# Where three kinds of sums are made: operands of a last product, weights' sums by DMA, and gated branch adds

## Chip, cores and metric

The kernel runs on one core of a Trainium2 chip. The metric is device time in microseconds, the median of three runs: 1693.74 us (1692.67 to 1696.91). All times below are microseconds (us) unless marked ns; times within an execution count from the start of its span.

## What is computed

Two layers of a transformer block over 512 tokens of width 1024, in float32. Each layer has a mixer of four branches (three kinds of attention and a retention), gated and summed, and then a gated feed-forward product:

```
h = rms_norm(x, g_pre_mix[l])
branches = stack(o_a, o_b, o_c, o_d)            # (S, 4, 256)
gates = sigmoid(h @ w_gate).reshape(S, 4, 1024)
merged = sum(einsum('snw,nwd->snd', branches, w_branch) * gates, axis=1)
x = x + rms_norm(merged @ w_out, g_post_mix[l])
h = rms_norm(x, g_pre_ffn[l])
f = (silu(h @ w_ffn_gate[l]) * (h @ w_ffn_up[l])) @ w_ffn_down[l]
x = x + rms_norm(f, g_post_ffn[l])
```

## The kernel before

**Matmuls in three.** Every float32 matrix is split into a high part in TensorE's own float format and a low part, the remainder. ScalarE casts the high part, VectorE (in a few places GpSimd) subtracts to get the low one, and TensorE does three matmuls: high by high, high by low, low by high. Weights come from HBM by DMA into `raw` tiles and are split into `whi` and `wlo`, four buffers each, two steps ahead of their use: `conversion` (lines 289 and 290) for most, `plain` (lines 403 and 404) in the feed-forward stage. Activations are split by `split_to` (lines 520 and 521, or 523 and 524 where a factor is applied).

**The gates** (`gates`). For each layer there are four groups, one per branch (`gi` 0 to 3), each with four pairs of 128 output columns (`dp` 0 to 3). A pair is two gate products of 24 matmuls, each followed by a multiplication on VectorE (line 1299) and a tanh on ScalarE (line 1300), and then two branch products of 6 matmuls. Their results are taken by line 1319 on VectorE, in place in the tanh's tile, and added to `merged` on GpSimd (line 1320). In the fourth group `merged` is final, and it is split at once for the output product (lines 523 and 524).

**Sums of weights** (`make_sums`). The last layer's down product, 2816 by 1024, is computed as a 2 by 2 block product with seven block products in place of eight. That needs four sums of weight blocks, p, r, q and v, for each of six k steps (`LAST_K`: five of two 128-row tiles, one of one). They are made in DRAM by DMAs that GpSimd issues, two for each sum: one copies (line 361), one adds (line 362), and q starts from p, v from q. Ahead of p and of r a DMA of one element (line 360) reads the tanh's tile just made, so that the sums start no earlier than that. One step's sums are made in each group with `gi` above 0, at its first pair: steps 0 to 2 in layer 0, 3 to 5 in layer 1 (step 5 is half as large). GpSimd issues in order, so its adds of line 1320 stand in one queue with these DMAs.

**The last product** (`finish`). It does the seven block products, P0 to P6 here, in six k steps each. The operands are quarters of the hidden matrix `h` (22 tiles; `FH` is 11) or sums of quarters. P0 takes one, P1 one, P2 the first sums (t1), P3 one, P4 the second sums (t2), P5 the third (t3), P6 the fourth (t4). `beside` makes t1 while P1 runs and t2 while P3 runs (lines 1753 and 1757, eleven adds each on 128 by 256). Those of t3 and t4 are made in `of_t3` and `of_t4` (lines 1783 and 1790), just ahead of the split of the same operand, which `operands(OPS)` calls three steps ahead of use. Each product has 66 matmuls (`block`, lines 1889 to 1891) into two banks, one for each 128 tokens of a half; the last two steps (`k` from `LATE` on) are done for the first bank and then for the second. P0, P4, P5 and P6 add into the same two banks, and so do P2 and P3 in two others. After a product, a copy on ScalarE (line 1837) takes each bank, VectorE adds it to another product's result (lines 1839, 1842, 1845), and `done` squares it (line 1815, with a sum), scales it (line 1817) and, at the end of a token's row, makes a root (`root`, line 551, for which ScalarE loads another function table) and writes the output (line 1828).

**The order of the work.** In the stages of the change no order is written by hand: a scheduler sets each engine's order when the program is built, and each engine then runs its instructions in that order, waiting where an operand or a buffer is not ready.

Of the kernel before, what the change touches and what calls it, by code (L numbers as in the profile page):

```python
# [13 lines left out]
ALU = mybir.AluOpType  # L14
# [22 lines left out]
HALF = (slice(0, 256), slice(256, 512))  # L37
# [18 lines left out]
FH = FT // 2  # L56
# [151 lines left out]
class Builder:  # L208
# [137 lines left out]
        return [self.ap["wts"][self.woff[i + j]:self.woff[i + j + 1]].rearrange("(p n) -> p n", p=128)  # L346
                for j in range(len(LAST_K))]

    def make_sums(self, j, when):

        dma = self.nc.gpsimd.dma_start
        a11, a12, a21, a22 = (self.block_quarter(n)[j] for n in range(4))
        n = a11.shape[1]
        for name, first, more in (("p", a21, a22), ("r", a11, a21), ("q", None, a11), ("v", None, a12)):
            d = self.dram.tile([128, n], F32, tag="%s%d" % (name, j), name="sums")
            self.sums[name, j] = d
            if first is None:
                first = self.sums["p" if name == "q" else "q", j]
            else:
                dma(d[0:1, 0:1], when[0:1, 0:1])  # L360
            dma(d, first, max_dma_last_dim=1024)
            dma(d, more, accum_op=ALU.add, max_dma_last_dim=1024)

# [926 lines left out]
    def gates(self, l, u):  # L1290
        nc = self.nc
        merged = [None] * 8
        for gi, n in enumerate(GATE_ORDER):
            for dp in range(4):
                ts = []
                for d in range(2):
                    ps = yield from self.fm("gate", u)
                    z = self.a()
                    nc.vector.tensor_mul(z, ps, self.rB)  # L1299
                    nc.scalar.activation(z, z, AF.Tanh, scale=0.5)  # L1300
                    ts.append(z)
                    if d == 0 and dp == 0 and gi > 0:
                        self.make_sums(3 * l + gi - 1, z)
                    yield 3
                if dp == 0:
                    self.drain("b%d" % n)
                br = self.br[n]
                w = self.take("branch")
                for d in range(2):
                    ps = self.ps("acc")  # L1310
                    for k in range(2):
                        self.mm3(ps, (w[0][2 * d + k], w[1][2 * d + k]), br[k], k == 0, k == 1)
                    dd = 2 * dp + d
                    if gi == 0:
                        merged[dd] = self.a()
                        nc.vector.scalar_tensor_tensor(merged[dd], ts[d], 1.0, ps, op0=ALU.add, op1=ALU.mult)
                    else:
                        t = ts[d]
                        nc.vector.scalar_tensor_tensor(t, t, 1.0, ps, op0=ALU.add, op1=ALU.mult)
                        nc.gpsimd.tensor_add(merged[dd], merged[dd], t)  # L1320
                    if gi == 3:
                        merged[dd] = self.split(merged[dd], scale=0.5)
                yield 12
        return merged
# [408 lines left out]
    def finish(self, h):  # L1733

        nc = self.nc
        h0, h1 = HALF
        mm = nc.tensor.matmul
        stt = nc.vector.scalar_tensor_tensor
        gout = [self.a(), self.a()]
        for i in range(2):  # L1740
            nc.sync.dma_start(gout[i], self.ap["gout"][:, 512 * i:512 * i + 512])
        t1, t2 = [None] * FH, [None] * FH
        row = lambda k: (k // 2, HALF[k % 2])

        def total(dst, k, f):

            i, hs = row(k)
            if k % 2 == 0:
                dst[i] = self.a()
            f(dst[i][:, hs])  # L1750
# [10 lines left out]
        def split(src, n):  # L1761
            hi, lo = self.ar(), self.ar()
            self.split_to(hi[:, :n], lo[:, :n], src[:, :n])
            return hi, lo

        def plain(k0, hs):
            def f(k, nk):
                hi, lo = self.ar(), self.ar()
                for i in range(nk):
                    self.split_to(hi[:, HALF[i]], lo[:, HALF[i]], h[k0 + k + i][:, hs])  # L1770
                return hi, lo
            return f

        def of_t1(k, nk):
            return split(t1[k // 2], 256 * nk)

        def of_t2(k, nk):
            return split(t2[k // 2], 256 * nk)

        def of_t3(k, nk):  # L1780
            t = self.a()
            for i in range(nk):
                nc.vector.tensor_sub(t[:, HALF[i]], h[FH + k + i][:, h1], h[k + i][:, h1])
                h[k + i] = None
            return split(t, 256 * nk)

        def of_t4(k, nk):
            t = self.a()
            for i in range(nk):
                stt(t[:, HALF[i]], t2[k // 2][:, HALF[i]], -1.0, h[FH + k + i][:, h0], op0=ALU.mult, op1=ALU.subtract)  # L1790
            t2[k // 2] = None
            return split(t, 256 * nk)

        products = (plain(0, h0), plain(FH, h0), of_t1, plain(FH, h1), of_t2, of_t3, of_t4)

        beside = {1: make_t1, 3: make_t2}
        todo = deque((f, k, nk) for f in products for k, nk in LAST_K)
        ready = deque()

# [212 lines left out]
```

## Time and profile before

| what | value |
|---|---|
| median of three runs | 1693.74 us (1692.67 to 1696.91) |
| profiled execution, own time | 1688.88 us |
| its span, first to last instruction | 1687.1 us |
| TensorE matmul (PE) busy | 1650.9 us, 98% |
| VectorE (DVE) busy | 1132.2 us, 67% |
| ScalarE (ACT) busy | 851.2 us, 50% |
| GpSimd (POOL) busy | 376.1 us, 22% |
| mean granted TensorE clock | 0.997 |

The profiled execution is a single one, with its own time beside the span. PE is matmul time, and matmuls overlap a little, so their starts say more than their durations. Issuing a DMA is not counted as busy. A wait is put down to the engine that came last by the profile; where that engine was itself held, the cause is one link further back.

### The profile page before, as it was taken

Reading aid. Unit: us, or ns where it says so; the run is one execution under the profiler, and the core shown is the slowest. Engines: PE = TensorE matmul, PEld = TensorE weight load, DVE = VectorE, ACT = ScalarE, POOL = GpSimd, SP = SyncE. Lnnn points to the kernel's source line nnn. Section 1 sums busy time; section 2 is a strip of 40 time slices with the busy share of each in tenths; the row PEclk is TensorE's granted clock in tenths of the full one; section 3 lists DMA queues with packets and bytes.
Section 4 is the critical chain, followed back from the end, with each engine's and each line's share of the span. In section 5 each row is a group of like instructions: output and inputs, shape, how many; then the busy total and the mean of one; then the engine's idle time right before and its main releaser. Section 6 shows DMA issues by size and latency. Waiting matters only on the chain.

```text
span 1687.1 us, 26433 instructions
## 1 busy us (share of the span) xinstructions
PE 1650.9 (98%) x9746; PEld 1460.2 (87%) x9746; DVE 1132.2 (67%) x2149; ACT 851.2 (50%) x1680; POOL 376.1 (22%) x404
## 2 busy tenths in 40 slices
PE   9999999999999999999999999999999999999997
PEld 7788888888798999988887888888888989999875
DVE  6667777644569777762286577675445687777987
ACT  6566553323455555553265665533334565555664
POOL 0145333332230000000121453334332300010000
PEclk9999999999999999999999999999999999999998
DMA  5644325776625777343236343257755257775561
GB/s 198 178 107 127 93 82 185 171 191 157 201 82 146 182 184 183 101 152 101 76 128 181 104 130 90 84 176 179 192 142 174 65 150 193 184 186 150 189 238 68
DMA packets 93313, 248.88 MB, mean 148 GB/s; under 512 B 11136, under 2 KB 22656, under 8 KB 93184
## 3 DMA queue, kind: packets, MB, share of 16 engines
q1 hardware_dynamic: 72768, 205.24, 38.8%
q0 software_dynamic: 20416, 41.95, 13.4%
q8 instruction: 77, 1.26, 0.3%
q14 instruction: 52, 0.43, 0.1%
HBM read 220.93 MB, written 31.46 MB: 150 GB/s over the span
## 4 chain that ended last, share of the span: by engine, by line
PE 59%; DVE 5%; ACT 2%; issue 1%; DMA 1%; POOL 1%; DVEq 0%; SPq 0%; ACTq 0%
PE acc L528 8%; PE acc L529 8%; PE acc L530 8%; PE acc L502 4%; PE acc L504 4%; PE acc L503 4%; PE b L504 3%; PE b L503 3%; PE b L502 3%; PE b L1889 1%; PE b L1891 1%; PE b L1890 1%; PE b L751 1%; DVE wlo L290 1%; PE b L671 1%
## 5 line engine op out<-in xcount | busy, mean ns | idle before, releaser
L528 PE MATMUL acc<-a,whi 128*128 128x512 f32 (+1 forms) x1238 | 477.8, 386 | 3.0 <-DVE a L1299 3.0
L530 PE MATMUL acc<-a,wlo 128*128 128x512 f32 (+1 forms) x1238 | 469.0, 379 | 0.0
L529 PE MATMUL acc<-a,whi 128*128 128x512 f32 (+1 forms) x1211 | 458.6, 379 | 0.0
L290 DVE TENSOR_TENSOR wlo<-raw,whi 128x512 fp32r<-128x512 f32 (+3 forms) x398 | 279.0, 732 | 134.1 <-ACT whi L289 133.3
L289 ACT CAST whi<-raw 128x512 fp32r<-128x512 f32 (+3 forms) x398 | 213.0, 576 | 305.8 <-PE acc L529 155.9
L530 PEld LDWEIGHTS acc<-a,wlo 128*128 128x128 f32 x1238 | 233.0, 188 | 44.0 <-issue 0.5
L528 PEld LDWEIGHTS acc<-a,whi 128*128 128x128 f32 x1238 | 233.9, 189 | 42.5 <-ACT whi L289 3.8
L529 PEld LDWEIGHTS acc<-a,whi 128*128 128x128 f32 x1211 | 228.5, 189 | 38.9 <-DVE a L524 0.6
L404 DVE TENSOR_TENSOR wlo<-raw,whi 128x1024 fp32r<-128x1024 f32 x132 | 157.6, 1195 | 71.2 <-ACT whi L403 67.7
L403 ACT CAST whi<-raw 128x1024 fp32r<-128x1024 f32 x132 | 135.4, 1027 | 122.7 <-PE acc L503 51.1
L502 PE MATMUL acc<-a,whi 128*128 128x256 f32 x560 | 158.6, 283 | 1.9 <-DVE a L1638 1.5
L503 PE MATMUL acc<-a,whi 128*128 128x256 f32 x560 | 158.4, 283 | 0.0
L504 PE MATMUL acc<-a,wlo 128*128 128x256 f32 x560 | 158.3, 283 | 0.0
L502 PE MATMUL b<-a,whi 128*128 128x256 f32 x448 | 126.8, 283 | 0.0
L503 PE MATMUL b<-a,whi 128*128 128x256 f32 x448 | 126.8, 283 | 0.0
L504 PE MATMUL b<-a,wlo 128*128 128x256 f32 x448 | 126.8, 283 | 0.0
L1299 DVE TENSOR_TENSOR a<-acc,a 128x512 f32<-128x512 f32 x64 | 44.1, 689 | 111.4 <-PE acc L530 111.4
L520 ACT CAST a<-a 128x512 fp32r<-128x512 f32 (+1 forms) x143 | 77.6, 567 | 74.7 <-DVE a L859 18.0
L333 POOL DMA_DIRECT2D raw<-wts x36 | 31.6, 877 | 350.1 <-DMA raw<-wts 129.0
L502 PEld LDWEIGHTS acc<-a,whi 128*128 128x128 f32 x560 | 107.4, 192 | 2.3 <-ACT whi L403 1.7
L503 PEld LDWEIGHTS acc<-a,whi 128*128 128x128 f32 x560 | 107.5, 192 | 0.1
L504 PEld LDWEIGHTS acc<-a,wlo 128*128 128x128 f32 x560 | 107.4, 192 | 0.0
(280 smaller groups left out, 3237.7 us busy)
## 6 DMA issues: line engine op xcount, KB each, us to landing
raw<-wts SPq DMA_DIRECT2D x257, 512.0 KB, 3.9
raw<-wts POOLq DMA_DIRECT2D x36, 512.0 KB, 6.5
a<-a SPq DMA_DIRECT2D x120, 128.0 KB, 2.3
sums<-wts POOLq DMA_DIRECT2D x30, 512.0 KB, 7.3
raw<-sums SPq DMA_DIRECT2D x20, 512.0 KB, 3.9
raw<-wts SPq DMA_DIRECT2D x35, 256.0 KB, 2.9
sums<-sums POOLq DMA_DIRECT2D x10, 512.0 KB, 4.6
a<-xT SPq DMA_DIRECT2D x16, 256.0 KB, 5.4
```

The lines of the kernel that those rows point to most:

```text
L289: todo.append(lambda hi=hi, src=src, n=n: nc.scalar.copy(hi[:, :n], src))
L290: todo.append(lambda hi=hi, lo=lo, src=src, n=n: (lo_engine or nc.vector).tensor_sub(lo[:, :n], src, hi[:, :n].bitcast(F32)))
L403: self.nc.scalar.copy(hi, src)
L404: self.nc.vector.tensor_sub(lo, src, hi.bitcast(F32))
L502: mm(o, hi[:, c], x[k][0], start=first, stop=False, skip_group_check=i in (2, 3, 4, 6))
L503: mm(o, hi[:, c], x[k][1], start=False, stop=False, skip_group_check=i in (2, 3, 4, 6))
L504: mm(o, lo[:, c], x[k][0], start=False, stop=k == 3, skip_group_check=i in (2, 3, 4, 6))
L520: nc.scalar.copy(hi, src)
L528: mm(out, w[0], x[0], start=start, stop=False)
L529: mm(out, w[0], x[1], start=False, stop=False)
L530: mm(out, w[1], x[0], start=False, stop=stop)
L1299: nc.vector.tensor_mul(z, ps, self.rB)
```

## The change

The one-element DMA now stands ahead of each of the four sums, and the four are made in two groups of four large DMAs: p and r at a group's first pair of columns, q and v at its third. In the fourth gate group the add to `merged` is on VectorE. The sums of t3 are made beside P2 and those of t4 beside P4, the latter in place in the tiles of t2.

```diff
-    def make_sums(self, j, when):
+    def make_sums(self, j, names, when):
...
         for name, first, more in (("p", a21, a22), ("r", a11, a21), ("q", None, a11), ("v", None, a12)):
+            if name not in names:
+                continue
             d = self.dram.tile([128, n], F32, tag="%s%d" % (name, j), name="sums")
             self.sums[name, j] = d
             if first is None:
                 first = self.sums["p" if name == "q" else "q", j]
-            else:
-                dma(d[0:1, 0:1], when[0:1, 0:1])
+            dma(d[0:1, 0:1], when[0:1, 0:1])
             dma(d, first, max_dma_last_dim=1024)
             dma(d, more, accum_op=ALU.add, max_dma_last_dim=1024)
...
-                    if d == 0 and dp == 0 and gi > 0:
-                        self.make_sums(3 * l + gi - 1, z)
+                    if d == 0 and dp % 2 == 0 and gi > 0:
+                        self.make_sums(3 * l + gi - 1, ("pr", "qv")[dp // 2], z)
...
-                        nc.gpsimd.tensor_add(merged[dd], merged[dd], t)
+                        (nc.vector if gi == 3 else nc.gpsimd).tensor_add(merged[dd], merged[dd], t)
...
-        def of_t3(k, nk):
-            t = self.a()
-            for i in range(nk):
-                nc.vector.tensor_sub(t[:, HALF[i]], h[FH + k + i][:, h1], h[k + i][:, h1])
-                h[k + i] = None
-            return split(t, 256 * nk)
-
-        def of_t4(k, nk):
-            t = self.a()
-            for i in range(nk):
-                stt(t[:, HALF[i]], t2[k // 2][:, HALF[i]], -1.0, h[FH + k + i][:, h0], op0=ALU.mult, op1=ALU.subtract)
-            t2[k // 2] = None
-            return split(t, 256 * nk)
...
+        def make_t3(k):
+            total(t3, k, lambda o: nc.vector.tensor_sub(o, h[FH + k][:, h1], h[k][:, h1]))
+            h[k] = None
+
+        def make_t4(k):
+
+            i, hs = row(k)
+            o = t2[i][:, hs]
+            stt(o, o, -1.0, h[FH + k][:, h0], op0=ALU.mult, op1=ALU.subtract)
...
-        beside = {1: make_t1, 3: make_t2}
+        beside = {1: make_t1, 2: make_t3, 3: make_t2, 4: make_t4}
```

Lines after the first edit have moved by one: what is line 403 before is 404 after, and so on. The order moves at three places.

GpSimd's queue in layer 0's fourth gate group, before; `sums` are the DRAM tiles of p, r, q and v, `a_2650` to `a_2897` are tiles of `merged`:

```order
L361 DMA sums_4221<-wts 512x256
L362 DMA sums_4217<-wts 512x256
L1320 TENSOR_TENSOR a_2650<-a_2650,a_4214 128x512
L362 DMA sums_4221<-wts 512x256
L361 DMA sums_4225<-sums_4217 512x256
L1320 TENSOR_TENSOR a_2659<-a_2659,a_4264 128x512
L362 DMA sums_4225<-wts 512x256
L361 DMA sums_4228<-sums_4225 512x256
L1320 TENSOR_TENSOR a_2888<-a_2888,a_4334 128x512
```

The same queue now:

```order
L361 DMA sums_4221<-a_4218 1x1
L361 DMA sums_4225<-a_4218 1x1
L362 DMA sums_4221<-wts 512x256
L362 DMA sums_4225<-wts 512x256
L363 DMA sums_4221<-wts 512x256
L363 DMA sums_4225<-wts 512x256
L361 DMA sums_4441<-a_4438 1x1
L361 DMA sums_4445<-a_4438 1x1
L362 DMA sums_4441<-sums_4221 512x256
```

The adds to `merged` have left the queue, and a second pair of one-element DMAs stands in it.

ScalarE from the end of P2, before; `whi` are the weights' high parts (the third to the sixth of P3 are `whi_17126` to `whi_17205`), `acc_16651` and `acc_16652` the two banks that P2 and P3 add into:

```order
L403 CAST whi_17076<-raw_16972 128x1024
L1837 COPY a_17089<-acc_16651 128x512
L403 CAST whi_17126<-raw_16994 128x1024
L1837 COPY a_17100<-acc_16652 128x512
L403 CAST whi_17153<-raw_17016 128x1024
L403 CAST whi_17180<-raw_17038 128x1024
L403 CAST whi_17205<-raw_17062 128x512
L520 CAST a_17118<-a_15674 128x256
```

And now, with the third weight of P3 as `whi_17155`:

```order
L404 CAST whi_17103<-raw_16984 128x1024
L521 CAST a_17095<-a_15442 128x256
L521 CAST a_17095<-a_15685 128x256
L404 CAST whi_17155<-raw_17009 128x1024
L1837 COPY a_17118<-acc_16663 128x512
L1837 COPY a_17129<-acc_16664 128x512
L404 CAST whi_17182<-raw_17034 128x1024
L404 CAST whi_17209<-raw_17059 128x1024
L404 CAST whi_17234<-raw_17086 128x512
```

The cast of P3's third weight has moved ahead of the first bank's copy.

ScalarE between P5 and P6, before; `whi_17538` to `whi_17632` are P6's second to fourth weights, `b_16647` and `b_16648` the banks:

```order
L403 CAST whi_17538<-raw_17426 128x1024
L520 CAST a_17496<-a_17494 128x256
L520 CAST a_17521<-a_17518 128x512
L403 CAST whi_17609<-raw_17451 128x1024
L403 CAST whi_17632<-raw_17476 128x1024
L520 CAST a_17534<-a_17531 128x512
L1837 COPY a_17551<-b_16647 128x512
L1815 ACTIVATE a_17554,sm16_16653<-a_17551 128x512
L1837 COPY a_17581<-b_16648 128x512
L551 ACT_TABLE_LOAD
```

And now, with P6's second to fourth weights as `whi_17555`, `whi_17623` and `whi_17643`:

```order
L404 CAST whi_17555<-raw_17457 128x1024
L1837 COPY a_17568<-b_16659 128x512
L1815 ACTIVATE a_17571,sm16_16665<-a_17568 128x512
L404 CAST whi_17623<-raw_17479 128x1024
L552 ACT_TABLE_LOAD
L552 ACTIVATE sm1_17577<-sm1_17575 128x1
L1837 COPY a_17598<-b_16660 128x512
L404 CAST whi_17643<-raw_17501 128x1024
L1815 ACTIVATE a_17601,sm16_16665<-a_17598 128x512
```

The first bank's copy has moved ahead of two weight casts; the second bank's copy has moved behind the table load. On TensorE, P6 now begins with two steps (12 matmuls) on the first bank before the second bank is used, where it was one step (6).

## Rows read from the trace of the kernel before

**Rows 1.** The page's first part: busy us, share of the span, instructions.

```profile
PE 1650.9 (98%) x9746; PEld 1460.2 (87%) x9746; DVE 1132.2 (67%) x2149; ACT 851.2 (50%) x1680; POOL 376.1 (22%) x404
```

**Rows 2.** Waits of PE, whole execution: line, releaser, us in total, times, longest.

```profile
PE b L1889 <- ACT a L1837: 3.1, 2, 2.7
PE acc L528 <- DVE a L1299: 3.0, 2, 2.0
```

**Rows 3.** Busy us by stretch: PE, PEld, DVE, ACT, POOL; then PEclk, DMA share, GB/s.

```profile
400.00:440.00 40.00, 36.97 (x163) 29.99 (x162) 19.58 (x32) 14.10 (x27) 14.44 (x14) 1.00 0.74 184
1240.00:1280.00 40.00, 40.00 (x178) 33.11 (x178) 22.88 (x36) 16.25 (x30) 13.82 (x14) 1.00 0.57 156
430.00:432.00 2.00, 0.14 (x1) 0.00 (x0) 1.32 (x3) 1.66 (x3) 0.00 (x0) 1.00 1.13 273
```

**Rows 4.** Timeline of POOL, layer 0's fourth group: start, us, what, idle before and releaser.

```profile
395.29 1.07 POOL L360 DMA_DIRECT2D sums<-a  x2 [4.71 <-ACT a L1300]
399.50 1.28 POOL L361 DMA_DIRECT2D sums<-wts  x2 [3.14 <-DMA sums<-a]
...
412.17 0.66 POOL L361 DMA_DIRECT2D sums<-sums  x1 [5.05 <-DMA sums<-wts]
412.83 1.31 POOL L1320 TENSOR_TENSOR a<-a 128x512 f32<-128x512 f32 x1
```

**Rows 5.** Timeline of ACT, the same group.

```profile
414.17 0.63 ACT L523 ACTIVATE a<-a 128x512 fp32r<-128x512 f32 x1 [7.47 <-POOL a L1320]
...
430.02 0.63 ACT L523 ACTIVATE a<-a 128x512 fp32r<-128x512 f32 x1 [3.09 <-POOL a L1320]
```

**Rows 6.** Timeline of PE in the last product.

```profile
1609.72 0.39 PE L1889 MATMUL acc<-whi,a 128*128 128x512 f32 x1
...
1616.35 0.50 PE L1889 MATMUL acc<-whi,a 128*128 128x512 f32 x1 [1.01 <-ACT a L520]
...
1647.18 0.50 PE L1889 MATMUL b<-whi,a 128*128 128x512 f32 x1 [0.36 <-ACT a L520]
...
1656.99 0.39 PE L1891 MATMUL b<-whi,a 128*128 128x512 f32 x1
1660.09 0.72 PE L1889 MATMUL b<-whi,a 128*128 128x512 f32 x1 [2.71 <-ACT a L1837]
...
1678.13 0.39 PE L1891 MATMUL b<-whi,a 128*128 128x512 f32 x1
```

**Rows 7.** Timeline of ACT in the last product.

```profile
1609.28 1.05 ACT L403 CAST whi<-raw 128x1024 fp32r<-128x1024 f32 x1 [0.81 <-PE acc L1891]
...
1656.53 0.62 ACT L520 CAST a<-a 128x512 fp32r<-128x512 f32 x1 [1.99 <-DVE a L1790]
1657.06 1.99 ACT L403 CAST whi<-raw 128x1024 fp32r<-128x1024 f32 x2
...
1659.47 0.57 ACT L1837 COPY a<-b 128x512 f32<-128x512 f32 x1
...
1663.26 1.28 ACT L551 ACT_TABLE_LOAD   x1
1664.56 0.20 ACT L551 ACTIVATE sm<-sm 128x1 f32<-128x1 f32 x1
```

**Rows 8.** Busy us by stretch after P6's first matmul, columns as in rows 3.

```profile
1661.00:1662.00 1.00, 1.00 (x4) 0.77 (x3) 1.00 (x2) 0.00 (x0) 0.00 (x0) 0.50 0.00 0
...
1664.00:1665.00 1.00, 1.00 (x6) 0.83 (x5) 0.90 (x3) 0.99 (x3) 0.00 (x0) 1.00 0.07 16
```

**Rows 9.** Timeline of DVE, layer 0's fourth group, first pair.

```profile
400.30 0.69 DVE L1319 SCALAR_TENSOR_TENSOR a<-a,acc 128x512 f32<-128x512 f32 x1
```

**Rows 10.** Timeline of DVE in the last product.

```profile
1610.37 1.23 DVE L404 TENSOR_TENSOR wlo<-raw,whi 128x1024 fp32r<-128x1024 f32 x1 [2.22 <-ACT whi L403]
...
1655.74 0.75 DVE L1790 SCALAR_TENSOR_TENSOR a<-a 128x256 f32<-128x256 f32 x2
```

**Rows 11.** All DMAs that write `sums`, one-element ones included: us from issue to landing.

```profile
DMA to landing us min/median/max: 2.5/4.6/10.4
```

More of the change, by code (lines that the diff above doesn't have):

```diff
@@ L1741, in finish @@
             nc.sync.dma_start(gout[i], self.ap["gout"][:, 512 * i:512 * i + 512])
-        t1, t2 = [None] * FH, [None] * FH
+        t1, t2, t3 = ([None] * FH for _ in range(3))
         row = lambda k: (k // 2, HALF[k % 2])
@@ L1772, in plain, with of, f @@
             return f
[L1774 to L1778, printed above, removed]
-        def of_t3(k, nk):
-            t = self.a()
-            for i in range(nk):
-                nc.vector.tensor_sub(t[:, HALF[i]], h[FH + k + i][:, h1], h[k + i][:, h1])
-                h[k + i] = None
-            return split(t, 256 * nk)
-        def of_t4(k, nk):
-            t = self.a()
-            for i in range(nk):
-                stt(t[:, HALF[i]], t2[k // 2][:, HALF[i]], -1.0, h[FH + k + i][:, h0], op0=ALU.mult, op1=ALU.subtract)
-            t2[k // 2] = None
-            return split(t, 256 * nk)
-        products = (plain(0, h0), plain(FH, h0), of_t1, plain(FH, h1), of_t2, of_t3, of_t4)
-        beside = {1: make_t1, 3: make_t2}
+        def make_t3(k):
[5 more added lines that the diff above has]
+            stt(o, o, -1.0, h[FH + k][:, h0], op0=ALU.mult, op1=ALU.subtract)
+        def of(t, last):
+            def f(k, nk):
+                src = t[k // 2]
+                if last:
+                    t[k // 2] = None
+                return split(src, 256 * nk)
+            return f
+        products = (plain(0, h0), plain(FH, h0), of(t1, False), plain(FH, h1), of(t2, False), of(t3, True),
+                    of(t2, True))
+        beside = {1: make_t1, 2: make_t3, 3: make_t2, 4: make_t4}
         todo = deque((f, k, nk) for f in products for k, nk in LAST_K)
```

## Prediction

> **What bounds the kernel now.** I read the busy shares first, then TensorE's waits, then its busy time by stretch, and last the single instructions around each gap. TensorE is busy for 98% of the span [rows 1], so only its gaps can be won by an edit that leaves the matmuls alone, as this one does. Over the whole execution its list of waits has two entries that touch the changed code: 3.0 us in two waits on line 1299 of the gates, and 3.1 us in two waits on line 1837 of the last product [rows 2]. The reader is to see that the engines named there (VectorE, ScalarE) are only the last link, and that something else held them.
>
> In the gates, the stretch of 400 to 440 us in layer 0 has 36.97 us of busy TensorE, 3.0 short of full, and the same stage of layer 1 (1240 to 1280 us) has 40.00 [rows 3]. The gap is made on GpSimd. The fourth gate group's DMAs for the weights' sums start at 395.29; a later one of them goes out at 412.17, after a wait for the landing of the one before it, and only then does the add of line 1320 start, at 412.83 [rows 4]. ScalarE's cast of that sum (line 523) stood 7.47 us idle for it, and a later one 3.09 us [rows 5]. Behind those casts in ScalarE's order stand the weights' casts that TensorE needs, hence the wait. Layer 1's fourth group moves half-size sums, and there TensorE does not wait.
>
> In the last product (P0 to P6), P6 is the slow one. P5's last matmul starts at 1656.99 and P6's first at 1660.09; P6's last starts at 1678.13 [rows 6]. Matmuls start 0.225 us apart when nothing waits (178 in 40.00 us, rows 3), so 66 of them are 14.8 us, and P6 took 1678.3 - 1657.2 = 21.1: an excess of 6.3. Why: ScalarE's operand cast at 1656.53 had waited 1.99 us for a fourth-operand sum (line 1790); two weight casts follow at 1657.06; and only at 1659.47 comes the copy (line 1837) that frees the bank for P6 [rows 7]. After that gap TensorE's granted clock is 0.50, which is 1.2 GHz, and by 1664 it is 1.00 again, 2.4 GHz [rows 8]; before it fell, the engine had stood still for 2.9 us. The earlier idle of nearly 2 us at 430 left the clock at 1.00 [rows 3].
>
> **The change part by part.** *Last gates add on VectorE.* Eight adds per layer leave GpSimd. On VectorE an add of this shape reads like line 1319's, 0.69 us [rows 9], so 5.5 us are added to a stretch where VectorE has 19.58 of 40 busy [rows 3]. VectorE does them in order behind the product that feeds them, so no DMA stands before ScalarE's cast any more. Nothing is queued behind them that TensorE lacks: a pair of branch products has two adds, 1.4 us, in a period of 13.6 us (60 matmuls). The merged tiles still come from GpSimd for the third group, but each is needed 54 us after its own add. Worth: the 3.0 us of layer 0, nothing in layer 1. Bounds: 0 if another hold replaces it, 3.1 with the slower first matmul after a gap.
>
> *Sums in groups of four DMAs.* Two more one-element DMAs per group, 12 in all, each pair issued in 1.07 us on GpSimd [rows 4], which nothing now waits for in the fourth group. What is new is a wait: line 1319 at the third pair of columns writes the tile that these DMAs read, so VectorE must wait for them, and line 290's weights stand behind it. At the first pair this wait exists today: the DMAs are issued at 395.29, their landing lets the next issue go at 399.50 [rows 4], and line 1319 starts at 400.30 [rows 9], so 0.8 us are spare. I cost it at nothing; the cover is that spare time, and without it see the last rival. The large DMAs are the same 48, spread over more of each group, and the last product reads their sums much later.
>
> *Third-operand sums beside P2.* Eleven half-width sums of 0.375 us (0.75 for two, rows 10) are 4.1 us more in P2's 14.8. VectorE has idle time there, 2.22 us before one weight conversion and more before others [rows 10], and the weights are converted two steps (5.4 us) ahead, so I cost the sums themselves at nothing. But the order changes on ScalarE: the cast of P3's third weight now stands ahead of both copies of line 1837 at the end of P2. That cast waits for TensorE to leave its buffer and runs 1609.28 to 1610.33 [rows 7]; the copy, 0.59 us, would end at 1610.9, while P3's first matmul, which adds to that bank, ran at 1609.72 [rows 6]. A new gap of 1.1 us (bounds: 0 if the cast gets its buffer earlier, 1.8 if both copies had to end). P3's own gap of 1.01 us at 1616.35 [rows 6] stays: there the last weight's cast still stands ahead of the operands' casts.
>
> *Fourth-operand sums beside P4.* They are another 4.1 us on VectorE, where four third-operand sums (1.5 us) leave P4's stretch. By the order, VectorE would come to P5's first weights about when it does now; cost nothing. In P5 the wait of 0.36 us at 1647.18 [rows 6] goes, since its operand's sum is long done: 0.4 gained. Between P5 and P6 the operand casts find their sums ready, and the copy for the first bank now stands before P6's third and fourth weight casts: that bank is free before P5 ends. What is late next is the second bank's copy. From the end of the first copy, 1.3 us before P5 ends (nine matmuls of 2.0 us follow, less a copy and its start), come an add on VectorE (0.6), a square (about the copy's 0.6), a weight cast (1.05), the table load (1.28), a root and the copy itself (0.6): 4.1 and some 0.6 of hand-overs, so it ends 3.4 after P5's end. TensorE, now ordered to do two steps of the first bank first, asks for it after 12 matmuls, 2.7 us: a wait of 0.7. No wait of this size has lowered the clock in rows 3, so the half clock goes too. P6 comes to 15.5 instead of 21.1: 5.6 gained (bounds: 3.0 if the clock still falls and operands are late by as much as a copy, 6.3 if nothing waits).
>
> On that table load: the row shows 1.28 us, and the root behind it starts at 1664.56, 0.02 us after its end [rows 7]. The Trainium skill (ScalarE: Activation LUTs, What ACT_TABLE_LOAD costs) puts every switch at about 2.66 us, a drain of 1.38 us included. By that the wait in P6 would be 2.1 us and the sum 1.4 us smaller. The measured row decides.
>
> **Sum.** -3.0 (gates) + 1.1 (P3) - 0.4 (P5) - 5.6 (P6) = -7.9 us. Against the profiled execution's own time (1688.88 us, span 1687.1) that is 1681.0; that execution is 4.9 us below the median of the runs shown, and I take the sum off the median: 1693.74 - 7.9 = **1685.8 us**. A measurement of this kernel tells about 0.3%, 5.1 us, from no change.
>
> **Rivals.** *New holds in the last product* (chance 0.15). The order of ScalarE decides, and it holds casts that wait for buffers ahead of copies at each product's end. For it: P3's new 1.1 us is of this kind. Against: VectorE's load per product is evened out. If half of P6's excess stays, the sum is -4.8: 1688.9. *The gates' gap does not go* (0.05): another late add or DMA holds ScalarE; against it, nothing else on its chain is late. Sum -4.9: 1688.8. *The table load costs more than its instruction* (0.10): if the copy behind it starts 1.4 us later than the root's start in rows 7 allows, the sum is -6.5: 1687.2. The trace speaks against it, as the root follows at once. This is what the Trainium skill's figure for a table switch (ScalarE: Activation LUTs) would do here.
>
> *Slower* (0.05): the one-element DMAs land behind the large ones of the same queue. Six new places hold VectorE, three per layer. The landing of these DMAs as a whole is 2.5 to 10.4 us [rows 11], and the wait bites from 5.0 us on (395.29 to 400.30). A hold of 7.47 us on ScalarE cost TensorE about 1.0 us, and the next, longer gap 2.0 us [rows 2, 5]. At 2.0 us in each of six places that is +12.0, and the total +4.1: 1697.8. Against: at the first pairs the DMAs land in time today, and by the third pair, 27 us later, the first two sums have landed.
>
> **How the numbers follow.** The forecast as summed has a chance of 0.65. The range: if neither new gap comes (1.1 and 0.7), the sum is -9.7, 1684.0, and the medians vary by 1 to 2 us (the lowest run is 1.1 below the median): low 1682.5. The high end takes in the three smaller gains and the same spread: 1690.0. Faster by over 0.3% needs a gain of 5.1: nearly all of the first case, most of the table case, under half of the two at 4.8 and 4.9: 0.77. Within 0.3%: 0.19. Slower by over 0.3%: 0.04.
>
> **What would show it.** Right: no wait of TensorE on line 1299 in layer 0's fourth group, and a full stretch there; in the last product, a gap of about 1 us at P3's start that is not there now, P6 near 15.5 us, granted clock 1.00 throughout, and the second copy of line 1837 behind the table load. Wrong: a wait of line 1319 on a DMA at the third pair of columns; a gap over 2 us between P5 and P6 with a clock of 0.50 behind it; weight conversions of P2 or P4 that end after TensorE asks for them.

## Result and profile after

The changed kernel took 1681.48 us (median of 4 runs, 1680.72 to 1685.04), beside 1693.28 us (4 runs, 1692.67 to 1696.91) for the kernel before: ratio 0.993, 95% interval 0.991 to 0.995. It is faster by over 0.3%, as forecast, but below the forecast range of 1682.5 to 1690.0. The two profiled executions lie nearer to each other: 1681.88 us (span 1680.1) after, 1688.88 (span 1687.1) before, so 7.0 apart, where the sum of the prediction was 7.9. In the stretches defined below these 7.0 are -3.7 (A), +1.4 (B) and -4.8 (C), to within 0.1.

The page's first part after has TensorE as busy as before [rows 1], in a shorter span:

```profile
PE 1651.0 (98%) x9746; PEld 1462.8 (87%) x9746; DVE 1134.5 (68%) x2165; ACT 849.8 (51%) x1680; POOL 360.8 (21%) x400
```

TensorE's waits over the whole execution no longer hold the gates' 3.0 us and the 3.1 us of [rows 2]. The line of the copies, 1837, now has a new wait of 1.0 at P3's start and one of 0.3 in P6:

```profile
PE acc L1889 <- ACT a L1837: 1.0, 1, 1.0
...
PE b L1889 <- ACT a L1837: 0.3, 1, 0.3
```

The two gate stretches of [rows 3], same columns, are now both full:

```profile
400.00:440.00 40.00, 40.00 (x178) 33.15 (x177) 24.31 (x41) 15.34 (x29) 6.63 (x9) 1.00 0.71 190
1240.00:1280.00 40.00, 40.00 (x178) 33.12 (x177) 25.07 (x42) 15.75 (x30) 6.80 (x10) 1.00 0.55 147
```

On ScalarE the casts that stood 7.47 and 3.09 us idle for a sum [rows 5] come in pairs. The timeline shows a pair's first without an idle time, and its second 1.12 us behind VectorE's add:

```profile
415.88 0.63 ACT L524 ACTIVATE a<-a 128x512 fp32r<-128x512 f32 x1
...
418.13 0.63 ACT L524 ACTIVATE a<-a 128x512 fp32r<-128x512 f32 x1 [1.12 <-DVE a L1321]
```

In the last product, the timeline of TensorE (its first matmul, P3's start, the wait in P3, P5's last matmul, the wait in P6, P6's last) is to be read beside [rows 6]:

```profile
1562.52 0.40 PE L1889 MATMUL b<-whi,a 128*128 128x512 f32 x1
...
1608.59 0.50 PE L1889 MATMUL acc<-whi,a 128*128 128x512 f32 x1 [0.99 <-ACT a L1837]
...
1615.39 0.50 PE L1889 MATMUL acc<-whi,a 128*128 128x512 f32 x1 [1.06 <-ACT a L521]
...
1655.53 0.39 PE L1891 MATMUL b<-whi,a 128*128 128x512 f32 x1
...
1658.96 0.50 PE L1889 MATMUL b<-whi,a 128*128 128x512 f32 x1 [0.33 <-ACT a L1837]
...
1671.11 0.39 PE L1891 MATMUL b<-whi,a 128*128 128x512 f32 x1
```

There is no wait in P5, and none ahead of P6. ScalarE's timeline (P3's third weight and the two copies; then the table load and the second bank's copy) is to be read beside [rows 7]:

```profile
1607.01 1.05 ACT L404 CAST whi<-raw 128x1024 fp32r<-128x1024 f32 x1 [1.78 <-issue]
1607.96 1.07 ACT L1837 COPY a<-acc 128x512 f32<-128x512 f32 x2
...
1656.94 1.28 ACT L552 ACT_TABLE_LOAD   x1
1658.24 0.20 ACT L552 ACTIVATE sm<-sm 128x1 f32<-128x1 f32 x1
1658.35 0.57 ACT L1837 COPY a<-b 128x512 f32<-128x512 f32 x1
```

The second copy stands behind the table load, as the order said, and costs TensorE 0.33 us. In the microseconds after that wait the clock stays whole, where [rows 8] had 0.50:

```profile
1660.00:1661.00 1.00, 1.00 (x6) 0.84 (x5) 1.00 (x2) 1.00 (x4) 0.00 (x0) 1.00 0.00 0
1661.00:1662.00 1.00, 1.00 (x6) 0.84 (x5) 1.00 (x4) 1.00 (x2) 0.00 (x0) 1.00 0.00 0
```

### The profile page after: what moved, and what is told of

The parts are those of the page before. It is cut to its first block, busy times and chain, and to the rows that moved or that the text cites. A ratio compares the mean times of both kernels' runs of the same rounds, so it can differ in the third digit from the quotient of the medians.

```text
span 1680.1 us, 26467 instructions
## 1 busy us (share of the span) xinstructions
PE 1651.0 (98%) x9746; PEld 1462.8 (87%) x9746; DVE 1134.5 (68%) x2165; ACT 849.8 (51%) x1680; POOL 360.8 (21%) x400
## 4 chain that ended last, share of the span: by engine, by line
PE 60%; DVE 4%; ACT 1%; issue 1%; DMA 1%; POOL 1%; SPq 0%; DVEq 0%; ACTq 0%
PE acc L529 8%; PE acc L530 8%; PE acc L531 8%; PE acc L503 4%; PE acc L505 4%; PE acc L504 4%; PE b L505 3%; PE b L504 3%; PE b L503 3%; PE b L1889 1%; PE b L1891 1%; PE b L1890 1%; PE b L752 1%; DVE wlo L290 1%; PE b L672 1%
## 5 line engine op out<-in xcount | busy, mean ns | idle before, releaser
L1300 DVE TENSOR_TENSOR a<-acc,a 128x512 f32<-128x512 f32 x64 | 44.2, 691 | 135.1 <-PE acc L531 131.6
```

## Experiments

**How they are read.** The runs of one kernel differ by up to 7.5 us (e1_before), more than most parts of this change are worth. So beside each ratio stand three stretches of the one profiled execution, each between two matmuls that every trace has:

- A, the gates of layer 0: from the matmul of line 697 that waits at about 222 us to the one of line 569 that waits at about 495 (lines 698 and 570 where lines moved by one).
- B, the attention of layer 1: from the matmul of line 697 behind the wait of 1.8 us at about 930 to the one that waits at about 1065.
- C, the last product: its first matmul to its last.

The two ends of A in TensorE's timeline of e1_before; A is 495.70 - 222.31 = 273.4:

```profile
222.31 0.33 PE L697 MATMUL b<-ct,a 128*128 128x128 f32 x1 [0.47 <-POOL a L690]
...
495.70 0.58 PE L569 MATMUL b<-ct,a 128*128 128x1 f32 x4 [0.39 <-DVE a L1531]
```

| kernel | median us (runs) | before, run beside it | ratio, 95% interval | A | B | C |
|---|---|---|---|---|---|---|
| before, first profile | | | | 272.6 | 135.0 | 113.4 |
| changed, first profile | 1681.48 (4) | 1693.28 (4) | 0.993, 0.991 to 0.995 | 268.9 | 136.4 | 108.6 |
| e1_before | 1689.54 (11) | 1690.98 (30) | 0.9998, 0.9987 to 1.0009 | 273.4 | 135.0 | 113.9 |
| e2_dve_add | 1686.80 (8) | 1690.98 (30) | 0.9972, 0.9962 to 0.9982 | 268.9 | 135.0 | 113.5 |
| e3_finish | 1686.82 (11) | 1690.98 (30) | 0.9977, 0.9969 to 0.9986 | 273.2 | 135.1 | 108.7 |
| e4_sums | 1688.73 (11) | 1690.98 (30) | 0.9982, 0.9973 to 0.9991 | 270.4 | 135.2 | 113.5 |
| e5_t3 | 1688.03 (11) | 1691.50 (17) | 0.9982, 0.9973 to 0.9991 | 273.4 | 135.0 | 111.1 |
| e6_t4 | 1687.00 (6) | 1691.50 (17) | 0.9968, 0.9956 to 0.9981 | 275.7 | 135.0 | 111.2 |
| e7_no_regroup | 1680.40 (5) | 1691.50 (17) | 0.9933, 0.9920 to 0.9945 | 268.9 | 135.0 | 108.5 |
| e9_after | 1682.37 (5) | 1691.50 (17) | 0.9936, 0.9924 to 0.9948 | 268.9 | 136.4 | 108.6 |
| e8_copy_dve | 1682.95 (6) | 1690.95 (11) | 0.9951, 0.9939 to 0.9963 | 268.9 | 136.4 | 108.7 |
| e10_best | 1681.88 (5) | 1690.95 (11) | 0.9943, 0.9931 to 0.9956 | 268.9 | 135.0 | 108.8 |
| e11_sums_dve | 1687.23 (10) | 1691.74 (15) | 0.9972, 0.9962 to 0.9983 | 268.9 | 136.4 | 113.9 |
| e12_no_regroup | 1680.80 (6) | 1691.74 (15) | 0.9937, 0.9923 to 0.9951 | 268.9 | 136.4 | 108.5 |

**e1_before**, the kernel before without an edit.

> The kernel before, unchanged, so that its profiled execution and its timed runs come from one chip. Theory A (the three parts gain what the two traces show, about 7.0, and the profiled execution of before was only a fast one): the timed median is again 1692 to 1694, and the gaps of TensorE in the new trace are those of the old one (3.0 at 414 to 432 in layer 0's fourth gate group, some 6 around P6), the span of the profiled execution anywhere from 1687 to 1692. Theory B (the edited places cost more in ordinary executions than in the one that was profiled): the new trace shows over 5 us idle in the fourth gate groups of both layers, or more than 6.3 us of excess in P6, and is 3 us or more longer than the old one. Theory C (time outside the edited places varies by 4 us): the new trace is longer, with the edited places unchanged.

Two things came out. Over 30 runs the median of the kernel before is 1690.98, not the 1693.74 of three runs; later sets of 17, 11 and 15 runs gave 1691.50, 1690.95 and 1691.74. So the three runs were high, and the first profiled execution (1688.88) lay within the spread of 1687.97 to 1694.77. Theory A's median of 1692 to 1694 did not come. Why the first runs were high stays open: of the 73 later runs on four chips, 17 were as high as the lowest of them (1692.67). And stretch A took 0.8 longer than in the first profile, though its one long wait, 2.14 us, is hardly longer than the longest of [rows 2], 2.0. The timeline of TensorE at that wait in e1_before: matmuls start 0.43 us apart behind it, not 0.225.

```profile
428.93 0.39 PE L530 MATMUL acc<-a,wlo 128*128 128x512 f32 x1
431.45 0.76 PE L528 MATMUL acc<-a,whi 128*128 128x512 f32 x1 [2.14 <-DVE a L1299]
432.01 0.63 PE L529 MATMUL acc<-a,whi 128*128 128x512 f32 x1
432.44 0.63 PE L530 MATMUL acc<-a,wlo 128*128 128x512 f32 x1
```

Busy time by stretch of e1_before (columns as in [rows 3]) says why: the clock fell to 0.50, which is 1.2 GHz, for some 3 us.

```profile
430.00:431.00 1.00, 0.00 (x0) 0.00 (x0) 0.99 (x2) 1.00 (x2) 0.00 (x0) 1.00 1.20 223
431.00:432.00 1.00, 0.55 (x1) 0.50 (x2) 1.00 (x3) 0.67 (x3) 0.00 (x0) 0.72 1.24 196
432.00:433.00 1.00, 1.00 (x4) 0.79 (x3) 1.00 (x2) 0.57 (x2) 0.00 (x0) 0.50 0.95 150
433.00:434.00 1.00, 1.00 (x4) 0.81 (x3) 1.00 (x4) 0.86 (x2) 0.00 (x0) 0.50 0.51 108
434.00:435.00 1.00, 1.00 (x4) 0.77 (x4) 1.00 (x3) 0.28 (x1) 0.49 (x1) 0.58 0.93 324
435.00:436.00 1.00, 1.00 (x6) 0.82 (x5) 1.00 (x1) 0.16 (x1) 1.00 (x2) 1.00 0.92 213
```

The same fall shows in e3_finish, e5_t3 and e6_t4, behind waits of 2.36, 2.52 and 3.03 us; in e6_t4 it lasts nearly 7 us, and A takes 275.7. Of the five traces with the old gates only the first had whole clock there, behind 1.99 us. Part of theory B holds: this place usually costs more than in the execution that I read. Its size does not hold in general: 0.8 here, and 3 us or more only in e6_t4 (3.1).

**e2_dve_add**, the add alone.

```diff
-                        nc.gpsimd.tensor_add(merged[dd], merged[dd], t)
+                        (nc.vector if gi == 3 else nc.gpsimd).tensor_add(merged[dd], merged[dd], t)
```

> Only the fourth gate group's adds to merged move to VectorE; sums and last product as before. Theory A: no idle TensorE at 400 to 440 us, 3.0 to 3.7 us faster than before. Theory B: 6 to 8 us faster. If the regrouping of the sums was needed for the gain (GpSimd's queue holding something else), less than 1 us faster.

Stretch A is 268.9, and 400 to 440 us is full:

```profile
400.00:440.00 40.00, 40.00 (x178) 33.15 (x177) 25.09 (x42) 15.96 (x30) 6.71 (x8) 1.00 0.80 204
```

The median is 4.2 us under that of before (by the interval 3.0 to 6.4). The five traces with the old gates have A at 272.6, 273.4, 273.2, 273.4 and 275.7, mean 273.7: the edit is worth 3.7 to 6.8, on the mean 4.8. Theory A's place, a little over its size.

**e3_finish**, the last product alone, with `make_t3` and `make_t4` as in the change.

```diff
-        beside = {1: make_t1, 3: make_t2}
+        beside = {1: make_t1, 2: make_t3, 3: make_t2, 4: make_t4}
```

> Only the sums of t3 beside P2 and of t4 beside P4; gates as before. Theory A: 5 us faster (1.1 lost at P3's start, 0.4 won in P5, 5.6 to 6.0 won in P6). Theory B (P6 of ordinary executions is longer than in the profiled one): 8 us or more faster. Rival of new holds: under 3 us faster, with a gap of over 1 us between P5 and P6.

C falls to 108.7, from 113.6 (the mean of the five traces with the old last product): 4.9. The median is 4.2 us lower (by the interval 2.4 to 5.2). Theory A holds.

**e4_sums**, the regrouping alone, with `make_sums` as in the change.

```diff
-                    if d == 0 and dp == 0 and gi > 0:
-                        self.make_sums(3 * l + gi - 1, z)
+                    if d == 0 and dp % 2 == 0 and gi > 0:
+                        self.make_sums(3 * l + gi - 1, ("pr", "qv")[dp // 2], z)
```

> Only the regrouping of the weights' sums (one-element DMA ahead of each, p and r at the first pair, q and v at the third); adds of the fourth group still on GpSimd. My prediction put no price on it. Theory A: within 1 us of before, the gap at 414 moves or shrinks since fewer DMAs stand ahead of GpSimd's adds, but q's and v's stand ahead of later ones. Theory C', that the regrouping itself carries the unexplained 4 us: 3 to 5 us faster. Rival (one-element DMAs hold VectorE's line 1319): 4 to 12 us slower.

A is 270.4, 3.3 under the mean of 273.7, and the median is 2.2 us under that of before (by the interval 1.5 to 4.6), between theories A and C'. Alone, the regrouping removes most of what the add removes: at the group's start fewer DMAs stand ahead of GpSimd's adds, and the second of these adds goes out at 408.37, where it went out at 412.83 before [rows 4]. The slower rival's hold of VectorE does not show. One wait remains, at the group's end:

```profile
449.41 0.50 PE L530 MATMUL acc<-a,whi 128*128 128x512 f32 x1 [1.19 <-DVE a L525]
```

It ends with a split on VectorE, which stood behind two subtractions of line 290 that ran while GpSimd made two adds. VectorE's timeline has such a pair of 128x512 subtractions without adds and then one beside GpSimd's adds; the third row is GpSimd's:

```profile
441.82 1.28 DVE L290 TENSOR_TENSOR wlo<-raw,whi 128x512 fp32r<-128x512 f32 x2
...
444.61 4.14 DVE L290 TENSOR_TENSOR wlo<-raw,whi 128x512 fp32r<-128x512 f32 x2
```

```profile
445.28 2.91 POOL L1321 TENSOR_TENSOR a<-a 128x512 f32<-128x512 f32 x2
```

Two subtractions take 1.28 us alone and 4.14 beside the adds: of these the first took 0.68, and the second, from 445.21 on, 3.54. The Trainium skill (SBUF — State Buffer, Who interferes with whom) says that a VectorE instruction with two SBUF inputs contends with a GpSimd instruction that reads SBUF; the trace agrees, with 3.54 in place of 0.68.

**e5_t3** and **e6_t4**, each one half of the last product's edit (`of_t4` as before in the first, `of_t3` in the second). The first line with a plus is e5's, the second e6's:

```diff
-        beside = {1: make_t1, 3: make_t2}
+        beside = {1: make_t1, 2: make_t3, 3: make_t2}
+        beside = {1: make_t1, 3: make_t2, 4: make_t4}
```

> Only the sums of t3 are made ahead, beside P2; those of t4 are still made just ahead of their split; gates as before. Theory A (P6's loss came from ScalarE's casts that waited for the sums of t4): P3 starts with a gap of 1 us that is new, P5 loses its 0.36, P6 keeps its gap of over 2 us and the half clock after it: within 1.5 us of before. Rival (what counts is how even VectorE's load is over the products, whichever sums move): half of the 4.2 us of both together, 2 us faster.

> Only the sums of t4 are made ahead, beside P4; those of t3 are still made just ahead of their split; gates as before. Theory A: no new gap at P3's start, P5's 0.36 stays or grows to 1 us since VectorE has both kinds of sums in P4, no gap over 1 us ahead of P6 and no half clock: 5 to 6 us faster. Rival (load of VectorE): 2 us faster, with new waits for operands or weights in P4 or P5.

C is 111.1 and 111.2, so each half alone gains 2.4 to 2.5 of the 5.0, as the rival said. But that is not half of P6. P6, from P5's last matmul to its own last, took 21.1 to 21.7 us in the traces with the old last product and takes 15.6 with both halves. With t3 alone it takes 18.14, with t4 alone 16.24:

```profile
1658.37 0.39 PE L1891 MATMUL b<-whi,a 128*128 128x512 f32 x1
...
1676.51 0.39 PE L1891 MATMUL b<-whi,a 128*128 128x512 f32 x1
```

```profile
1664.70 0.39 PE L1892 MATMUL b<-whi,a 128*128 128x512 f32 x1
...
1680.94 0.39 PE L1892 MATMUL b<-whi,a 128*128 128x512 f32 x1
```

So in P6 theory A is nearly right for t4, which brings 4.9 to 5.4 us there, and wrong for t3, which it gave nothing and which brings 3.0 to 3.5. The two overlap. What evens the totals is paid elsewhere: t3 alone has the new gap at P3's start, and t4 alone makes P5, from P4's last matmul to its own last, 18.99 us long, where it was 16.3 before and is 15.4 with t3. With t3 alone, ScalarE's timeline still has waits for fourth-operand sums in P6, and TensorE loses 0.48, 0.67 and 0.36 us in three waits; but the first bank's copy now stands ahead of the weight casts, no wait in P6 reaches 1 us, and the clock holds.

```profile
1668.48 0.62 ACT L520 CAST a<-a 128x512 fp32r<-128x512 f32 x1 [3.02 <-DVE a L1790]
...
1671.85 0.62 ACT L520 CAST a<-a 128x512 fp32r<-128x512 f32 x1 [2.75 <-DVE a L1790]
```

With t4 alone, P4 and P5 carry both kinds of sums; TensorE (timeline) waits 1.63 us in P5 and 0.98 in P6, and behind the first the clock is 0.50 from 1655 to 1658. That execution was the slowest of the six runs of e6_t4 (1691.72), whose median is 4.5 us under that of before; how often the clock falls there is not known from one trace.

```profile
1653.27 0.50 PE L1890 MATMUL b<-whi,a 128*128 128x512 f32 x1 [1.63 <-ACT a L520]
...
1666.07 0.50 PE L1890 MATMUL b<-whi,a 128*128 128x512 f32 x1 [0.98 <-ACT a L1838]
```

**e7_no_regroup**, the diffs of e2 and e3 together and so the sums in the old grouping; **e9_after**, the changed kernel again.

> The changed kernel without the regrouping of the weights' sums: adds of the fourth group on VectorE, sums of t3 and t4 beside P2 and P4. Theory A (with the adds on VectorE nothing waits behind GpSimd's DMAs, so the regrouping is worth nothing more): 8.5 to 9.5 us faster than before, within 1 us of the changed kernel. Rival (the regrouping is worth the 2 us that it gave alone): 6 to 7 us faster.

> The changed kernel again, beside the same runs of the kernel before as the others. Theory A (4.2 to 4.5 from the gates and 5.0 from the last product, and nothing else): 8.7 to 9.5 us faster than before, so 1681 to 1682. Rival (the 11.8 us of the first comparison, with a further gain somewhere): 11 us or more.

The medians are 11.1 and 9.1 us under 1691.5, the intervals overlap nearly whole, and A and C are the same: where the adds are on VectorE, the regrouping gains nothing that these runs can tell, as theory A of e7_no_regroup said, though its 11.1 is above the 8.5 to 9.5 of that theory. The changed kernel's 9.1 is in theory A's range of e9_after. A and C account for 4.8 + 5.0 = 9.8 us; the 1.4 that B takes back in its traces leaves 8.4.

**e8_copy_dve**, the changed kernel with P2's copies on VectorE; **e10_best**, the same on e7's edits.

```diff
-                    nc.scalar.copy(s, ps)
+                    (nc.vector.tensor_copy if n == 2 else nc.scalar.copy)(s, ps)
```

> The changed kernel with the two copies at the end of P2 on VectorE in place of ScalarE. Theory A (the new gap of 0.99 at P3's start is the copies behind the third weight's cast in ScalarE's order): the gap goes, and the last product, from its first matmul to its last, takes 107.6 in place of 108.6 us; the time 1 us shorter than the changed kernel's, 10 us shorter than before. Rival (the two copies, 0.7 us each, hold VectorE's weight conversions of P3): the gap only moves to later matmuls of P3, and the last product takes 108.4 to 109.

> The same two copies on VectorE, with the adds of the fourth group on VectorE and the sums of t3 and t4 made ahead, but the weights' sums in their old grouping. Theory A (the regrouping gains nothing where the adds are on VectorE, and costs nothing): as e8_copy_dve, the last product 107.6 us, the gates of layer 0 268.9 us, the time 10 us shorter than before. Rival (the fall of the clock at 927 us in layer 1, 1.4 us, which both traces of the changed kernel show and no other, comes with the regrouping): this one has 135.0 us of attention in layer 1 and e8_copy_dve 136.4.

The gap did not go; it grew from 0.99 to 1.31. VectorE's timeline and TensorE's wait in e8_copy_dve:

```profile
1604.99 1.22 DVE L405 TENSOR_TENSOR wlo<-raw,whi 128x1024 fp32r<-128x1024 f32 x1
1606.13 0.42 DVE L1776 TENSOR_TENSOR a<-a 128x256 f32<-128x256 f32 x1
1606.46 1.28 DVE L1837 COPY a<-acc 128x512 f32<-128x512 f32 x2
```

```profile
1607.30 0.47 PE L1889 MATMUL acc<-whi,a 128*128 128x512 f32 x1 [1.31 <-DVE a L1837]
```

P2's last matmul started at 1605.60; on VectorE the copies stand behind a weight conversion and a sum of t3, and start 0.9 later. C is 108.7 and 108.8: no gain. Theory A falls, and its rival holds in C. So no version here beats the changed kernel clearly; e7's is as fast with less. In B the two kernels came out as the rival of e10_best said, 136.4 and 135.0, hence the next pair.

**e11_sums_dve**, the diffs of e2 and e4 together, without the last product's edit; **e12_no_regroup**, e7's kernel a second time. They ask why B took 136.4 in every trace that had both the regrouping and the adds, and 135.0 in the others.

> The regrouped sums and the adds on VectorE, without the edit of the last product. Theory A: gates of layer 0 268.9 us as with the adds alone, so no more than the adds alone gained (4.2 to 4.7 us faster than before), last product 113.5 us. Theory R (the regrouping brings the fall of the clock at 927 us in layer 1): attention of layer 1 136.4 us with half clock behind the 1.8 us wait on line 698. Rival (that fall is chance): 135.0 us there, full clock.

> A second execution of e7_no_regroup (adds on VectorE, sums of t3 and t4 ahead, old grouping). Theory R: 135.0 us in the attention of layer 1, full clock at 927 us, and 1 to 2 us faster than the changed kernel's 9.1. Rival (chance): the attention may take 136.4 us here too, and the time is that of the changed kernel, 9 us faster than before. Both theories: gates of layer 0 268.9 us, last product 108.6 us.

e11 has 136.4, but so has e12, without the regrouping, where e7 had 135.0 with the same program. So the fall does not need the regrouping, and one program can have it or not: theory R as stated falls. That the regrouping has no part in it is not shown: all four traces with both the regrouping and the adds had the fall, and one of the ten others. As to time, e11's median is 4.5 us under that of before, no more than the adds alone gained, and e12's is 10.9 under. Stretches 927 to 935 us, behind the same wait of 1.82 us, first in e7_no_regroup, then in e12_no_regroup:

```profile
927.00:935.00 8.00, 8.00 (x44) 6.56 (x45) 6.29 (x23) 6.90 (x19) 5.15 (x7) 1.00 0.29 67
```

```profile
927.00:935.00 8.00, 7.96 (x35) 6.62 (x36) 4.93 (x17) 5.57 (x16) 3.88 (x6) 0.79 0.21 49
```

## Why the prediction was right and wrong

The time missed the range by 1.0 us. Two terms failed.

**The base.** "that execution is 4.9 us below the median of the runs shown, and I take the sum off the median": the median was that of three runs, and 30 runs put it at 1690.98, 2.8 lower. From that base the sum gives 1683.1, inside the range. The profiled execution's own time less the sum, 1681.0, was 0.5 from the result, which is luck: that execution was 2.1 below the median, and this made up for a gates' term that was 1.8 too small. The runs differ where the change is not: from the start to the wait at 222 us the traces took 221.0 to 224.1, from 851 to 930 us 77.3 to 80.1, and B 135.0 or 136.4.

**The gates' -3.0.** The place and the cause were right (e2: A 268.9, the stretch full). The size was the idle time of one execution, with an upper bound of 3.1. Even there, start to start, A shrank by 3.7; and in the four other traces with the old gates the clock fell behind the wait, a cost that the bound left out. On the mean it is 4.8. The remark that an idle of nearly 2 us left the clock at 1.00 rested on that one execution. With both terms as measured, 1691.0 + 1.1 - 0.4 - 5.6 - 4.8 = 1681.3. That this lies so near to the two medians of the changed kernel, 1681.48 and 1682.37, is in part luck, as the 1.4 of B in both its traces is in no term.

One link of that step was read wrong. "Behind those casts in ScalarE's order stand the weights' casts that TensorE needs, hence the wait": in the trace of before the hold passes through VectorE's order. Its split (line 524) waited for ScalarE's cast, its multiplication (line 1299) stood behind that split, and TensorE waited for the multiplication:

```profile
430.68 0.69 DVE L524 SCALAR_TENSOR_TENSOR a<-a 128x512 fp32r<-128x512 f32 x1 [2.94 <-ACT a L523]
431.29 0.68 DVE L1299 TENSOR_TENSOR a<-acc,a 128x512 f32<-128x512 f32 x1
```

```profile
432.12 0.47 PE L528 MATMUL acc<-a,whi 128*128 128x512 f32 x1 [1.99 <-DVE a L1299]
```

The edit removes the start of the chain, GpSimd's late add, so the gain did not depend on this link.

**The last product, point by point.** Its first matmul is at 1562.52 after; before it was at 1564.77.

- P3's start: 1608.59 - 1562.52 = 46.07 us from that, 44.95 before; so 1.1 as forecast, behind the cast of the third weight as said.
- P5: the wait of 0.36 is gone. The sum's 0.4 is right by luck: P5 as a whole is 0.8 shorter (16.25 to 15.43), and P3 behind its start is 0.5 longer (16.30 to 16.78).
- P6: from P5's last matmul to P6's last, 1671.11 - 1655.53 = 15.58 us; 15.5 forecast, 21.14 before. The second bank's wait was 0.33 where I put 0.7, and no half clock followed.
- Together -4.8 in the first pair of traces and -5.0 on the mean (113.6 to 108.6), -4.9 forecast. The step's account of P6 named the fourth operand's sums alone; e5 shows that moving t3's alone also takes 3.0 to 3.5 us off P6, and in e6, without t3's move, P5 lost 2.7.

**What was costed at nothing.** VectorE took the adds and sums without a new hold: no wait of TensorE for a weight conversion in P2 or P4. The first GpSimd row is the second pair of one-element DMAs of layer 0's fourth group, the second the next issue, which their landing lets go; line 1320 (1319 before) started at 427.77, 1.0 later, and waited for nothing of it. In the whole execution VectorE's 13 waits ahead of line 1320 were all put down to TensorE. So the slower rival did not bite.

```profile
422.76 1.06 POOL L361 DMA_DIRECT2D sums<-a  x2 [15.19 <-ACT a L1301]
426.75 0.64 POOL L362 DMA_DIRECT2D sums<-sums  x1 [2.93 <-DMA sums<-a]
```

**The table rival** fell: the load took 1.28, the root started 0.02 after it and the copy followed at 1658.35, 0.13 after the load's end. All 13 loads of that execution took 1.28, with ScalarE's next instruction at most 0.02 behind each. The Trainium skill's figure of about 2.66 us for a switch (ScalarE: Activation LUTs, What ACT_TABLE_LOAD costs) shows nowhere here.

## What to carry to other kernels

Take a sum off a base made of many runs, and not off a median of three; a single profiled execution can lie on either side (here 2.1 below the median, in e6_t4 4.7 above). Look for stretches that differ between executions before the range is set. Cost a wait of TensorE start to start, and add the price of a half clock wherever the wait is near 2 us, even if the one trace at hand does not show it. An engine that holds another by its order (GpSimd's DMAs ahead of an add, ScalarE's casts ahead of a copy) was relieved here by making the operand earlier or elsewhere; moving the held instruction to a queue where other work stands ahead of it (e8) only moved the wait.

## What the hardware showed that was not expected

- Whether TensorE's clock falls behind a wait is not settled by the wait's length. Behind the wait of 1.82 us at 927 us, at the same place of the program, it fell in 5 of 14 traces and stayed whole in 9, at 1.4 us a fall (B); behind 1.99 us in the gates it held, behind 2.14 to 3.03 it fell in all four; behind 1.63 us in P5 it fell in e6_t4. What decides between the cases is open, and so is why four of the five falls at 927 us are in the four traces with both the regrouping and the adds on VectorE.
- Two subtractions on VectorE slowed from 1.28 to 4.14 us beside GpSimd's adds (e4_sums). So an add that leaves GpSimd also gives VectorE time back: in the changed kernel's gates the 128x512 subtractions of line 290 never took over 0.69 us in 395 to 445 us, where one took 1.46 before.
